# A gated convolution layer on one Trainium2 core: six tiles for the output weights, fourteen seven-product pairs, and sums made early

## The chip, the cores and the metric

The kernel runs on one core of one Trainium2 chip. The metric is the device time of one execution, in microseconds. The core has five engines that matter here: TensorE (PE) multiplies, VectorE (DVE) and ScalarE (ACT) work element by element, GpSimd (POOL) does small sums, and SyncE (SP) issues most of the transfers. A queue of an engine is worked off in the order in which it was written.

## What is computed

```python
D, E, T = 2048, 4096, 256            # model width, branch width, tokens; one sequence, one layer
h = rmsnorm(x, norm_g)
shift, scale, gate = split(silu(c) @ ada_w + ada_b, 3)
h = h * (1 + scale) + shift
b_gate, c_gate, v, g = split(h @ w_in, 4)        # w_in: D x 4E
u = causal_depthwise_conv(c_gate * v, conv_w)    # three taps
y = b_gate * u * silu(g)
out = rmsnorm(x + gate * (y @ w_out), final_g)   # w_out: E x D
```

All inputs and outputs are float32.

## The kernel before

**Products.** A float32 product is made of three matmuls in the type fp32r. Both operands are split into a high part (a cast, on ScalarE) and a low part (what the cast left out, a subtraction on VectorE), and high times high, high times low and low times high are added up. In the code a weight block `raw` gives `hi` (`split_hi`, line 380) and `lo` (`split_lo`, line 385). All weights are streamed from HBM in tiles of 128 x 2048 (1 MB). Three kinds of tile, called raw, hi and lo, exist three times each; `w_tile(kind, name)` hands them out in turn, and an engine that writes one waits until the last reader of its former contents is done. How tiles are handed out, and the order of each engine's instructions, is settled when the program is built: a list scheduler goes by the written order and by times of its own, and may put an instruction that it takes for ready ahead of an earlier one.

**Stages.** In the first 376 us the first half of the input projection runs while the adaptive norm's scale and shift are computed (matmuls `mm_s`). From 376 to 724 us the second half runs (`mm_b`): 8 groups of two channel tiles by 4 quarters (`QUARTERS`) by 2 blocks of `w_in`, 64 blocks of 48 matmuls. In its first half the gate's share of `ada_w` is streamed beside it, one `gate_piece` a block, and summed on VectorE and, over the partitions, on POOL; the bias comes into the two `gates` tiles at the stage's start, and POOL adds the sums to it. After the fourth quarter of a group `y` is ready, split into high and low part (`split_y`), as pair `ct // 2` of the 16 pairs of channel tiles.

**The output stage** multiplies `y` by `w_out` and runs from 724 us to the end. The first 1024 columns go first (`columns`, tiles `wide`), for the pairs in the given order; then the next 1024 columns (`halves`) for 12 of the pairs, while the last 8 channel tiles (`LAST`, two groups of `EP = 4`) are handled 512 columns at a time, the last 512 columns with the weights multiplied by the gate beforehand (`gated_piece`), so that their sum can go straight to the final row. A plain pair is 8 block products, two channel tiles by two token tiles by two column blocks of 512: 24 matmuls of 512 columns.

**Seven products.** For the pairs in `SEVEN` a scheme with seven block products takes the place of the eight, 21 matmuls. It needs sums of token blocks (`token_forms`, made when the pair's `y` is) and sums of weight blocks, which `seven` makes on VectorE (lines 837, 843 and 844) in a tile of kind lo. Such a pair uses two raw, two hi and two lo tiles: its own blocks 1 to 3 and the four sums. Its intermediate products pile up in the banks `p1`, `p6` and `p75`, and `gather` adds them up behind the last such pair. Before the change there are 6 such pairs in the first half (10 to 15) and 4 in the second (10 to 13). `tc.add_manual_dep` puts a pair's first sum behind the low part of the pair in front.

In the output stage the raw weights and the sums lie in the three tiles of kind lo, and the low parts in those of kind raw. The large buffer `big`, which holds the tokens until the last input product, then takes the residual `x` (`xr`), the row of final gains (`fg`) and a scratch row (`u2`); `load_ends` issues these loads behind pairs 4 to 6 of the order. At the end `residual`, `weighted` and `finish` apply gate, residual and norm and store the rows.

Of the kernel before, what the change touches and what calls it, by code (L numbers as in the profile page):

```python
# [13 lines left out]
P = 128  # L14
D = 2048
# [102 lines left out]
def short_conv_layer(ctx: ExitStack, tc: tile.TileContext, x, c, norm_g, ada_w, ada_b, w_in, conv_w, w_out, final_g, out):  # L118
# [553 lines left out]
    for j in range(2):  # L672
        nc.sync.dma_start(
            gates[j].rearrange("p a f -> p (a f)"),
            ada_b[0:1, 2 * D + j * 1024 : 2 * D + (j + 1) * 1024].partition_broadcast(P),
        )

    def gate(dc):
        return gates[dc // 2][:, dc % 2, :]

    gate_todo = [(dc, j) for dc in range(4) for j in range(0, KT, 2)]
    gacc = [None]
# [35 lines left out]
    ended_silu = [None]  # L718

    def token_forms(pair, u):  # L720

        sums = zs[0][:, 1].rearrange("p a (b f) -> p (a b) f", f=P)
        a11, a12 = u[:, 0, 0:P], u[:, 1, 0:P]
        a21, a22 = u[:, 0, P:T], u[:, 1, P:T]
        s1n, s2, s3, s4 = (sums[:, j] for j in range(4))
        nc.vector.scalar_tensor_tensor(out=s1n, in0=a21, scalar=-1.0, in1=a22, op0=ALU.mult, op1=ALU.subtract)
        nc.vector.scalar_tensor_tensor(out=s2, in0=s1n, scalar=-1.0, in1=a11, op0=ALU.mult, op1=ALU.subtract)
        nc.vector.tensor_tensor(out=s3, in0=a11, in1=a21, op=ALU.subtract)
        nc.vector.tensor_tensor(out=s4, in0=a12, in1=s2, op=ALU.subtract)
# [10 lines left out]
        nc.vector.tensor_tensor(out=lo, in0=sums, in1=hi.bitcast(F32), op=ALU.subtract)  # L740

    for ct in range(NS, NCT, 2):
        for q in QUARTERS:
            bank = psum.tile([P, CT, T], F32, tag="mm", name="mm_b")[:, 0:2]
            col = q * E + ct * P
            for kp in range(0, KT, KP):
# [6 lines left out]
                for m in range(2):  # L753
                    for i in range(KP):
                        k = kp + i
                        o = slice((i * 2 + m) * P, (i * 2 + m + 1) * P)
                        for j in range(3):
                            product(bank[:, m, :], hi[:, o], lo[:, o], k, j, k == 0 and j == 0, m == 0, k == KT - 1 and j == 2)
                gate_piece()
            z = zs[q // 2][:, q % 2]  # L760
            if q == 1:
                nc.scalar.copy(z, bank)
# [9 lines left out]
            else:  # L772
                nc.vector.tensor_tensor(out=u, in0=bank, in1=u, op=ALU.mult)
                split_y(ys[ct // 2], u)
                if ct // 2 in SEVEN:
                    token_forms(ct // 2, u)
    while gate_todo:
        gate_piece()


    W = 512
    big = hpool.tile([P, 3 * D + W], F32, tag="big", name="big")
    xr = big[:, 0 : TT * D].rearrange("p (t f) -> p t f", t=TT)
    fg = big[:, TT * D : 3 * D]
    u2 = big[:, 3 * D :]
    ends = [z.rearrange("p a b f -> p (a b f)").rearrange("p (h f) -> p h f", h=2) for z in zs]

    def load_ends(n):

        if 0 <= n < TT:  # L790
            nc.sync.dma_start(xr[:, n, :], x[n * P : (n + 1) * P, :])
        elif n == TT:
# [9 lines left out]
    def load_o(raw, e0, ne, c0, n):  # L802
        nc.sync.dma_start(
            raw.rearrange("p (k f) -> p k f", k=ne),
            w_out[0, e0 * P : (e0 + ne) * P, c0 : c0 + n].rearrange("(k p) f -> p k f", p=P),
        )

    def y_parts(ct, t):
        return [ys[ct // 2][:, ct % 2, h, t * P : (t + 1) * P] for h in range(2)]
# [6 lines left out]
    def residual(t, c0, n, src, pr):  # L816


        r = xr[:, t, c0 : c0 + n]
        g = gates[c0 // 1024].rearrange("p a f -> p (a f)")[:, c0 % 1024 : c0 % 1024 + n]  # L820
        nc.vector.tensor_tensor(out=pr, in0=src, in1=g, op=ALU.mult)
        nc.vector.tensor_tensor(out=r, in0=r, in1=pr, op=ALU.add)

    def weighted(t, c0, n, pr, at):


        r = xr[:, t, c0 : c0 + n]
# [3 lines left out]
    def seven(j, raw, bank, p1, p6, p75, opens, last):  # L831


        sums = w_tile("lo", "sums_o")
        hi, lo = hi_tile(), lo_tile("raw")
        b, s, bh, bl = (v.rearrange("p (b f) -> p b f", f=W) for v in (raw, sums, hi, lo))
        first = nc.vector.tensor_tensor(
            out=s[:, 0:2], in0=b[:, 1:3], in1=b[:, 0:1].to_broadcast([P, 2, W]), op=ALU.subtract
        )
        if last_low[0] is not None:  # L840
            tc.add_manual_dep(first.ins, last_low[0].ins.name, after, reason="the pair in front comes first")
        nc.scalar.copy(bh[:, 1:4], b[:, 1:4])
        nc.vector.tensor_tensor(out=s[:, 2], in0=b[:, 2], in1=s[:, 0], op=ALU.add)
        all_sums = nc.vector.tensor_tensor(out=s[:, 3], in0=b[:, 3], in1=s[:, 2], op=ALU.subtract)
        low = nc.vector.tensor_tensor(out=bl[:, 1:4], in0=b[:, 1:4], in1=bh[:, 1:4].bitcast(F32), op=ALU.subtract)
        tc.add_manual_dep(low.ins, all_sums.ins.name, after, reason="the sums' cast runs beside the low part")
        sh, sl = (v.rearrange("p (b f) -> p b f", f=W) for v in split(sums, SLOT, "raw"))
# [19 lines left out]
        add(ends[0][:, 0], p75[:, 1], u2)  # L867
        add(ends[1][:, 0], p75[:, 1], ends[1][:, 1])

    def columns(c0, order, sevens, bank, p1, p6, p75, whole, loads=None):  # L870
# [26 lines left out]
    def wide_bank(name):  # L897
# [2 lines left out]
    p75 = wide_bank("mm_7")  # L900
    wide = [wide_bank("mm_w") for _ in range(TT)]
    columns(
        0, (0, 1, 10, 2, 11, 3, 12, 4, 13, 5, 14, 6, 15, 7, 8, 9), SEVEN,
        lambda t, d: wide[t][:, d], *extra_banks(), p75, True, load_ends,
    )
    for t in range(TT):
        c = ends[t].rearrange("p h f -> p (h f)")
# [7 lines left out]
    def finish(t):  # L915
# [3 lines left out]
        nc.vector.reciprocal(fs, fs)  # L919
        for c0, n, vector in ((0, 512, True), (512, 512, False), (1536, 512, True), (1024, 512, False)):  # L920
            dd = slice(c0, c0 + n)
            r = xr[:, t, dd]
            if c0 == 1536:
                nc.vector.scalar_tensor_tensor(out=r, in0=po[t], scalar=fs, in1=fg[:, dd], op0=ALU.mult, op1=ALU.mult)
            elif vector:
# [2 lines left out]
                nc.scalar.activation(r, r, AF.Copy, scale=fs)  # L928
            nc.sync.dma_start(out[t * P : (t + 1) * P, dd], r)

    halves = [wide_bank("mm_o") for _ in range(2)]
    p75 = wide_bank("mm_7")
    LAST = (3, 4)
# [17 lines left out]
    def move(t):  # L951
# [5 lines left out]
        nc.vector.tensor_tensor(out=c, in0=c, in1=xr[:, t, 3 * W : 4 * W], op=ALU.add)  # L957
        nc.scalar.copy(po[t], c)

    def gated_piece(ep):  # L960
        raw = w_tile("lo", "raw_o")
        load_o(raw, ep * EP, EP, 3 * W, W)
        raw3 = raw.rearrange("p (k f) -> p k f", k=EP)
        nc.vector.tensor_tensor(out=raw3, in0=raw3, in1=gate(3).unsqueeze(1).to_broadcast([P, EP, W]), op=ALU.mult)
        return raw

    def third(t):
# [53 lines left out]
```

## Time and profile before

| | us |
|---|---|
| median of three runs | 901.92 (900.71, 901.92, 902.15) |
| span of the profiled execution, first to last instruction | 898.9 |
| its time outside the span | not listed; the span is 3.0 below the median |
| PE busy | 886.5 |
| DVE busy | 674.4 |
| ACT busy | 484.0 |
| POOL busy | 95.6 |

In the rows quoted below, PE is TensorE's matmuls, DVE is VectorE, ACT ScalarE, SPq the queue of transfers that SyncE issues; L385 is line 385 of the kernel. A row of a group gives line, engine, operation, what is written and read with its shape, how often, then the busy time in us, the mean of one in ns, and the idle time ahead of it with what ended it. A row of waits gives who waited for whom, in total, how often, and the longest. A row of the chain and of the timeline gives start and length in us; a matmul's length there contains a modelled end, so that one matmul's price is read from start to start. A row of the chain of work that ended last has how many matmuls followed each other without a gap.

### The profile page before, as it was taken

What the parts mean: (1) busy time and instruction counts of PE and PEld (TensorE: products, weight loads), DVE (VectorE), ACT (ScalarE), POOL (GpSimd) and SP (SyncE); (2) the same over time, 40 slices, a digit from 0 to 9 for tenths busy, and PEclk for the clock granted to TensorE, in tenths of its full rate; (3) what the DMA queues carried; (4) which work ended last, traced back from release to release, by engine and by line L of the source; (5) the groups of instructions that cost most, each with busy time, mean ns of one, the idle gap of its engine ahead of it and who ended that gap; (6) DMA issues with size and microseconds to landing.
All of it is one profiled execution on the core that took longest, in us unless ns stands there. A gap on an engine that the chain in (4) does not pass through costs nothing.

```text
span 898.9 us, 16428 instructions
## 1 busy us (share of the span) xinstructions
PE 886.5 (99%) x6989; PEld 849.7 (95%) x6989; DVE 674.4 (75%) x667; ACT 484.0 (54%) x430; POOL 95.6 (11%) x107
## 2 busy tenths in 40 slices
PE   7999999999999999999999999999999999999996
PEld 4999999999999999999999999999999988888885
DVE  5899988899888866755965677565555578879896
ACT  6768866665558856644433444443434445554543
POOL 0000001010000134024134103410000000000000
PEclk9999999999999999999999999999999999999998
DMA  9999999999998597687888789766666476674662
GB/s 309 369 369 368 369 336 361 347 365 367 372 318 291 167 277 231 196 266 244 278 246 242 252 273 274 233 207 204 193 188 188 141 290 224 192 276 126 202 234 94
DMA packets 160250, 235.53 MB, mean 262 GB/s; under 512 B 7028, under 2 KB 105924, under 8 KB 159792
## 3 DMA queue, kind: packets, MB, share of 16 engines
q1 hardware_dynamic: 156368, 226.52, 76.8%
q0 software_dynamic: 3680, 7.92, 3.2%
q8 instruction: 55, 0.90, 0.4%
q14 instruction: 19, 0.16, 0.0%
q10 hardware_dynamic: 128, 0.04, 0.0%
HBM read 224.49 MB, written 2.10 MB: 252 GB/s over the span
## 4 chain that ended last, share of the span: by engine, by line
PE 97%; DMA 2%; SPq 0%; ACT 0%; issue 0%; ACTq 0%; DVE 0%
PE mm_s L545 39%; PE mm_b L545 39%; PE mm_w L814 7%; PE mm_o L814 7%; PE mm L814 4%; DMA at<-in_ada_w_dram 2%; PE sum L418 0%; SPq L240 0%; PE tp_g L530 0%; PE tp_g L526 0%; ACT big L928 0%; ACTq L1017 0%; ACT fs L918 0%; ACT z L991 0%; DVE fs L919 0%
## 5 line engine op out<-in xcount | busy, mean ns | idle before, releaser
L545 PE MATMUL mm_b<-hT,hi 128*128 128x256 f32 x2048 | 348.2, 276 | 0.0
L545 PE MATMUL mm_s<-hT,hi 128*128 128x256 f32 x2048 | 335.6, 277 | 0.0
L545 PEld LDWEIGHTS mm_b<-hT,hi 128*128 128x128 f32 x2048 | 308.1, 188 | 0.0
L545 PEld LDWEIGHTS mm_s<-hT,hi 128*128 128x128 f32 x2048 | 299.0, 188 | 0.2
L545 PE MATMUL mm_b<-hT,lo 128*128 128x256 f32 x1024 | 282.6, 276 | 0.0
L545 PE MATMUL mm_s<-hT,lo 128*128 128x256 f32 x1024 | 261.3, 276 | 0.0
L385 DVE TENSOR_TENSOR lo<-raw,hi 128x2048 fp32r<-128x2048 f32 (+1 forms) x66 | 152.4, 2311 | 103.1 <-ACT hi L380 102.6
L380 ACT CAST hi<-raw 128x2048 fp32r<-128x2048 f32 (+1 forms) x66 | 123.7, 1874 | 192.7 <-PE mm_b L545 146.6
L545 PEld LDWEIGHTS mm_b<-hT,lo 128*128 128x128 f32 x1024 | 192.2, 188 | 0.0
L545 PEld LDWEIGHTS mm_s<-hT,lo 128*128 128x128 f32 x1024 | 182.4, 188 | 0.0
L385 DVE TENSOR_TENSOR lo<-raw_s,hi 128x2048 fp32r<-128x2048 f32 (+1 forms) x80 | 149.1, 1871 | 34.7 <-ACT hi L380 34.2
L380 ACT CAST hi<-raw_s 128x2048 fp32r<-128x2048 f32 (+2 forms) x81 | 124.1, 1541 | 61.7 <-PE mm_s L545 46.7
L515 DVE SCALAR_TENSOR_TENSOR gv<-at,silu_c,gv 128x512 f32<-128x512 f32 x105 | 79.0, 752 | 5.5 <-DMA at<-in_ada_w_dram 3.6
L568 ACT COPY acc<-mm_s 128x1024 f32<-128x1024 f32 x54 | 54.6, 1012 | 37.0 <-PE mm_s L545 37.0
L385 DVE TENSOR_TENSOR lo<-raw_o,hi 128x2048 fp32r<-128x2048 f32 x22 | 50.4, 2290 | 22.9 <-ACT hi L380 22.9
L380 ACT CAST hi<-raw_o 128x2048 fp32r<-128x2048 f32 x22 | 42.0, 1908 | 45.8 <-DMA raw_o<-in_sc_w_out_dram 12.3
L814 PE MATMUL mm_w<-hi,y 128*128 128x512 f32 x184 | 58.8, 389 | 0.0
L710 POOL TENSOR_TENSOR gacc<-gacc,z 128x512 f32<-128x512 f32 x28 | 45.6, 1628 | 106.8 <-DMA z<-gacc 106.8
L814 PE MATMUL mm_o<-hi,y 128*128 128x512 f32 x176 | 55.3, 389 | 0.0
L704 DVE SCALAR_TENSOR_TENSOR gacc<-at_g,silu_c,gacc 128x512 f32<-128x512 f32 x60 | 46.9, 782 | 6.0 <-DMA at_g<-in_ada_w_dram 4.8
L814 PEld LDWEIGHTS mm_w<-hi,y 128*128 128x128 f32 x184 | 34.5, 188 | 7.2
L582 ACT COPY mm_s<-acc 128x1024 f32<-128x1024 f32 x38 | 38.6, 1017 | 2.6 <-DVE acc L571 1.8
(161 smaller groups left out, 670.8 us busy)
## 6 DMA issues: line engine op xcount, KB each, us to landing
raw<-in_sc_w_in_dram SPq DMA_DIRECT2D x64, 1024.0 KB, 5.8
raw_s<-in_sc_w_in_dram SPq DMA_DIRECT2D x47, 1024.0 KB, 7.9
raw_o<-in_sc_w_out_dram SPq DMA_DIRECT2D x32, 1024.0 KB, 5.2
at<-in_ada_w_dram SPq DMA_DIRECT2D x126, 256.0 KB, 7.8
raw_s<-in_sc_w_in_dram SPq DMA_DIRECT2D x33, 512.0 KB, 7.3
at_g<-in_ada_w_dram SPq DMA_DIRECT2D x32, 512.0 KB, 8.0
x<-in_x_dram SPq DMA_DIRECT2D x4, 512.0 KB, 6.2
big<-in_x_dram SPq DMA_DIRECT2D x2, 1024.0 KB, 8.2
```

The source lines that it names most:

```text
L380: nc.scalar.copy(hi[:, :n], raw[:, :n])
L385: last_low[0] = nc.vector.tensor_tensor(out=lo[:, :n], in0=raw[:, :n], in1=hi[:, :n].bitcast(F32), op=ALU.subtract)
L515: nc.vector.scalar_tensor_tensor(out=gv, in0=at4[:, i], scalar=c_k, in1=gv, op0=ALU.mult, op1=ALU.add)
L545: mm = last_mm[0] = nc.tensor.matmul(dst, w, h[k], start=begins and left, stop=ends, skip_group_check=True)
L568: nc.scalar.copy(acc[ch, q], bank)
L582: nc.scalar.copy(bank, acc[ch, q])
L704: nc.vector.scalar_tensor_tensor(out=ga, in0=at3[:, i, :], scalar=s, in1=ga, op0=ALU.mult, op1=ALU.add)
L710: nc.gpsimd.tensor_tensor(out=ga, in0=ga, in1=turned, op=ALU.add)
L814: nc.tensor.matmul(dst, y[a], b, start=opens and i == 0, stop=ends and i == 2, skip_group_check=True)
```

## The change

- `SEVEN` becomes 8 to 15 in the first half, and `SEVEN_2`, 10 to 15, holds in the second: 14 seven-product pairs for 10. The orders of the pairs change. The token forms of pairs 8 and 9 lie in the two gate tiles.
- For that the gate leaves these tiles: it is kept as a row in HBM (`gate_row`), POOL's last sum of each quarter is added to it by an accumulating transfer, and `load_gate` fetches it in two halves, at the 11th and 14th pair (counted from 0) of the first half.
- In the first 1024 columns raw weights and sums go round six tiles (`wide_ring`): the three of kind lo, and three more in `big`, up to the 13th pair. From then `x` (first 1024 columns) and `fg` are loaded there. In the second half there are four (`next_ring`), the fourth in `big`, until twelve were handed out; then the second half of `x` is loaded there, at the 8th pair.
- `early_weights`, called behind each of the 64 blocks of the second input stage, makes the weight sums of pairs 10 to 15 for the second half (blocks 35, 39, ... 55) and the two gated pieces (blocks 59 and 62, the gate's last quarter being fetched at 58): load, VectorE, and a store to HBM on ACT's queue one block later. In the output stage they are loaded, with blocks 1 to 3 of the raw weights; the sums and the multiplication by the gate go out of that stage.
- `LAST` is (2, 3) and no longer (3, 4).

```diff
-    gates = [slot([P, 2, 512], f"gate{j}") for j in range(2)]
+    gate_slots = [slot([P, 2, 4, P], f"gate{j}", F32R) for j in range(2)]
...
+    gate_row = dram.tile([1, D], F32, tag="gate_row", name="gate_row")
+    nc.gpsimd.dma_start(gate_row, ada_b[0:1, 2 * D : 3 * D])
...
+    def load_gate(j):
+        c0 = j * 1024
+        nc.sync.dma_start(gate_columns(c0, 1024), gate_row[0:1, c0 : c0 + 1024].partition_broadcast(P))
...
-            nc.gpsimd.tensor_tensor(out=gate(dc), in0=ga, in1=gate(dc), op=ALU.add)
+            nc.gpsimd.dma_start(gate_row[0:1, dc * 512 : (dc + 1) * 512], ga[0:1], accum_op=ALU.add)
...
-    SEVEN = range(10, 16)
+    SEVEN = range(8, 16)
+    SEVEN_2 = range(10, 16)
...
-        if pair < 14:
+        if pair < 10:
+            form = gate_slots[pair - 8]
+            hi, lo = form[:, 0], form[:, 1]
+        elif pair < 14:
...
+    LAST = (2, 3)
+    EARLY = {35 + 4 * i: j for i, j in enumerate(SEVEN_2)}
+    EARLY.update({58: "gate", 59: ("gated", LAST[0]), 62: ("gated", LAST[1])})
+    def sums_of(b, s):
+        yield nc.vector.tensor_tensor(
+            out=s[:, 0:2], in0=b[:, 1:3], in1=b[:, 0:1].to_broadcast([P, 2, W]), op=ALU.subtract
+        )
+        yield nc.vector.tensor_tensor(out=s[:, 2], in0=b[:, 2], in1=s[:, 0], op=ALU.add)
+        yield nc.vector.tensor_tensor(out=s[:, 3], in0=b[:, 3], in1=s[:, 2], op=ALU.subtract)
+    def early_weights():
+        while to_store:
+            unit, sums = to_store.pop()
+            made[unit] = dram.tile([P, SLOT], F32, tag=f"made{len(made)}", name="made")
+            nc.scalar.dma_start(made[unit], sums)
+        unit = EARLY.get(passed[0])
+        passed[0] += 1
+        if unit is None:
+            return
+        if unit == "gate":
+            nc.sync.dma_start(turned, gate_row[0:1, 3 * W : 4 * W].partition_broadcast(P))
+            return
+        raw, sums = raw_tile("raw_u"), w_tile("lo", "sums_u")
+        blocks, out = (v.rearrange("p (b f) -> p b f", f=W) for v in (raw, sums))
+        if not isinstance(unit, int):
+            load_o(raw, unit[1] * EP, EP, 3 * W, W)
+            nc.vector.tensor_tensor(out=out, in0=blocks, in1=turned.unsqueeze(1).to_broadcast([P, EP, W]), op=ALU.mult)
+        else:
+            load_o(raw, 2 * unit, 2, 2 * W, 2 * W)
+            list(sums_of(blocks, out))
+        to_store.append((unit, sums))
...
                 gate_piece()
+                early_weights()
...
+    places6 = [None] * 3 + [big[:, i * SLOT : (i + 1) * SLOT] for i in range(3)]
+    taken, ending = [0], [False]
+    def wide_ring(name):
+        i = taken[0] % 6 if not ending[0] else 0
+        taken[0] += 1
+        return w_tile("lo", name) if places6[i] is None else places6[i]
     def load_ends(n):
+        ending[0] = n >= AT_END
+        if n == AT_END - 2:
+            load_gate(0)
+        elif n == AT_END:
+            load_x(0)
+        elif n == AT_END + 1:
             nc.sync.dma_start(fg, final_g.rearrange("(o d) -> o d", o=1).partition_broadcast(P))
+            load_gate(1)
...
+    AT_END = 13
...
-            raw = w_tile("raw" if n == 0 and c0 == 0 else "lo", "raw_o")
-            load_o(raw, 2 * j, 2, c0, 2 * W)
+            raw = w_tile("raw", "raw_o") if n == 0 and c0 == 0 else ring("raw_o")
+            ready = c0 > 0 and j in made
+            if ready:
+                blocks = raw.rearrange("p (b f) -> p b f", f=W)
+                e = 2 * j * P
+                nc.sync.dma_start(blocks[:, 1], w_out[0, e : e + P, c0 + W : c0 + 2 * W])
+                nc.sync.dma_start(blocks[:, 2:4].rearrange("p b f -> p (b f)"), w_out[0, e + P : e + 2 * P, c0 : c0 + 2 * W])
+            else:
+                load_o(raw, 2 * j, 2, c0, 2 * W)
             if loads:
-                loads(n - 4)
+                loads(n)
             if j in sevens:
-                seven(j, raw, bank, p1, p6, p75, j == sevens[0], j == sevens[-1])
+                sums = ring("sums_o")
+                if ready:
+                    nc.sync.dma_start(sums, made[j])
+                seven(j, raw, sums, ready, bank, p1, p6, p75, j == sevens[0], j == sevens[-1])
...
-        0, (0, 1, 10, 2, 11, 3, 12, 4, 13, 5, 14, 6, 15, 7, 8, 9), SEVEN,
+        0, (0, 1, 8, 2, 9, 3, 10, 4, 11, 5, 12, 13, 6, 14, 15, 7), SEVEN,
...
+    AT_X = 8
+    def next_ring(name):
+        i = taken[0] % 4
+        taken[0] += 1
+        return big[:, SLOT : 2 * SLOT] if i == 3 and taken[0] <= 12 else w_tile("lo", name)
...
-        2 * W, (0, 1, 2, 10, 3, 11, 4, 12, 5, 13, 14, 15), SEVEN[0:4],
-        lambda t, d: halves[d][:, t], *po, p75, False,
+        2 * W, (0, 1, 10, 2, 11, 3, 12, 13, 8, 14, 15, 9), SEVEN_2,
+        lambda t, d: halves[d][:, t], *po, p75, False, lambda n: load_x(1) if n == AT_X else None, next_ring,
...
     def gated_piece(ep):
         raw = w_tile("lo", "raw_o")
-        load_o(raw, ep * EP, EP, 3 * W, W)
-        raw3 = raw.rearrange("p (k f) -> p k f", k=EP)
-        nc.vector.tensor_tensor(out=raw3, in0=raw3, in1=gate(3).unsqueeze(1).to_broadcast([P, EP, W]), op=ALU.mult)
+        nc.sync.dma_start(raw, made["gated", ep])
         return raw
```

More of the change, by code (lines that the diff above doesn't have):

```diff
@@ L776, in short_conv_layer, with xr, load_x @@
                     token_forms(ct // 2, u)
+    early_weights()
     while gate_todo:
         gate_piece()
-    W = 512
     big = hpool.tile([P, 3 * D + W], F32, tag="big", name="big")
-    xr = big[:, 0 : TT * D].rearrange("p (t f) -> p t f", t=TT)
+    xh = big[:, 0 : TT * D].rearrange("p (h t f) -> p h t f", h=2, t=TT)
+    HD = D // 2
+    def xr(t, c0, n):
+        return xh[:, c0 // HD, t, c0 % HD : c0 % HD + n]
+    def load_x(h):
+        for t in range(TT):
+            nc.sync.dma_start(xh[:, h, t], x[t * P : (t + 1) * P, h * HD : (h + 1) * HD])
     fg = big[:, TT * D : 3 * D]
@@ L816, in residual, with seven @@
     def residual(t, c0, n, src, pr):
-        r = xr[:, t, c0 : c0 + n]
-        g = gates[c0 // 1024].rearrange("p a f -> p (a f)")[:, c0 % 1024 : c0 % 1024 + n]
-        nc.vector.tensor_tensor(out=pr, in0=src, in1=g, op=ALU.mult)
+        r = xr(t, c0, n)
+        nc.vector.tensor_tensor(out=pr, in0=src, in1=gate_columns(c0, n), op=ALU.mult)
         nc.vector.tensor_tensor(out=r, in0=r, in1=pr, op=ALU.add)
     def weighted(t, c0, n, pr, at):
-        r = xr[:, t, c0 : c0 + n]
+        r = xr(t, c0, n)
         nc.scalar.activation(pr, r, AF.Square, scale=D**-0.5, accum_out=fsq[:, t, at : at + 1])
         nc.vector.tensor_tensor(out=r, in0=r, in1=fg[:, c0 : c0 + n], op=ALU.mult)
-    def seven(j, raw, bank, p1, p6, p75, opens, last):
-        sums = w_tile("lo", "sums_o")
+    def seven(j, raw, sums, ready, bank, p1, p6, p75, opens, last):
         hi, lo = hi_tile(), lo_tile("raw")
         b, s, bh, bl = (v.rearrange("p (b f) -> p b f", f=W) for v in (raw, sums, hi, lo))
[L837 to L844, printed above, removed]
+        steps = [] if ready else sums_of(b, s)
+        all_sums = last_low[0]
+        for i, step in enumerate(steps):
+            if i == 0:
+                tc.add_manual_dep(step.ins, last_low[0].ins.name, after, reason="the pair in front comes first")
+                nc.scalar.copy(bh[:, 1:4], b[:, 1:4])
+            all_sums = step
+        if ready:
+            nc.scalar.copy(bh[:, 1:4], b[:, 1:4])
         low = nc.vector.tensor_tensor(out=bl[:, 1:4], in0=b[:, 1:4], in1=bh[:, 1:4].bitcast(F32), op=ALU.subtract)
@@ L902, in short_conv_layer @@
     columns(
-        0, (0, 1, 10, 2, 11, 3, 12, 4, 13, 5, 14, 6, 15, 7, 8, 9), SEVEN,
-        lambda t, d: wide[t][:, d], *extra_banks(), p75, True, load_ends,
+        0, (0, 1, 8, 2, 9, 3, 10, 4, 11, 5, 12, 13, 6, 14, 15, 7), SEVEN,
+        lambda t, d: wide[t][:, d], *extra_banks(), p75, True, load_ends, wide_ring,
     )
@@ L921, in finish @@
             dd = slice(c0, c0 + n)
-            r = xr[:, t, dd]
+            r = xr(t, c0, n)
             if c0 == 1536:
@@ L956, in move @@
         nc.vector.tensor_tensor(out=c, in0=c, in1=gate(3), op=ALU.mult)
-        nc.vector.tensor_tensor(out=c, in0=c, in1=xr[:, t, 3 * W : 4 * W], op=ALU.add)
+        nc.vector.tensor_tensor(out=c, in0=c, in1=xr(t, 3 * W, W), op=ALU.add)
         nc.scalar.copy(po[t], c)
```

33 lines of the change are left out of this document (17 added, 16 removed).

## The prediction

> **What bounds the kernel now.** I read the page first, then what TensorE waited for, then the chain that ended last.
>
> ```profile
> span 898.9 us, 16428 instructions
> PE 886.5 (99%) x6989; PEld 849.7 (95%) x6989; DVE 674.4 (75%) x667; ACT 484.0 (54%) x430; POOL 95.6 (11%) x107
> PE   7999999999999999999999999999999999999996
> DVE  5899988899888866755965677565555578879896
> raw_o<-in_sc_w_out_dram SPq DMA_DIRECT2D x32, 1024.0 KB, 5.2
> ```
>
> ```profile
> PE tp_v L274 <- DMA rows<-in_c_dram: 4.2, 1, 4.2
> PE sum L418 <- DMA at<-in_ada_w_dram: 0.4, 1, 0.4
> PE tp_x L335 <- ACT xs L341: 0.3, 1, 0.3
> PE sum L418 <- DVE mod L448: 0.3, 1, 0.3
> ```
>
> TensorE is busy for 886.5 of 898.9 us, and its waits (the second fence is all of them) are 5.2 us in total, all of the start-up. From the first product to the last nothing keeps it waiting, so only fewer matmuls, or a new stall, can move the time. VectorE is the next engine: the fifth row of the page shows it at 8 to 9 tenths in the last eight slices, which are the output stage that the change rewrites.
>
> ```profile
> 375.88 348.16 PE mm_b L545 x3072
> 724.04 10.89 PE mm_w L814 x48
> 790.27 16.79 PE mm_w L814 x74
> 807.07 16.32 PE mm_o L814 x72
> 880.81 10.89 PE mm L814 x48
> ```
>
> The output stage runs from 724.04 to 880.81 + 10.89 = 891.70 us. One matmul of 512 columns costs 10.89 / 48 = 0.2269 us from start to start. In the first 1024 columns the kernel issues 10 plain pairs of 24 matmuls and 6 seven-product pairs of 21, 366 in all: 366 x 0.2269 = 83.04 us, and the chain has 807.07 - 724.04 = 83.03. In the second half 8 x 24 + 4 x 21 + 48 + 48 = 372 give 84.4 against 84.6. So the matmul count alone gives the length, without a gap. A pair costs 5.44 us plain and 4.76 us with seven products.
>
> **The gain.** Seven-product pairs go from 6 to 8 in the first half and from 4 to 6 in the second: 360 + 366 matmuls instead of 366 + 372. Twelve fewer are 12 x 0.2269 = 2.72 us, or 0.30%. Nothing else lies on the path, since the tail behind the last matmul is not edited. The rest of the working asks what of the 2.72 us is given back.
>
> **VectorE in the first half.** The rows are mean durations in the output stage.
>
> ```profile
> L385 DVE TENSOR_TENSOR lo<-raw_o,hi 128x2048 fp32r<-128x2048 f32 x17 | 38.9, 2289 | 12.8 <-ACT hi L380 12.8
> L385 DVE TENSOR_TENSOR lo<-sums_o,hi 128x2048 fp32r<-128x2048 f32 x7 | 16.0, 2291 | 2.3 <-ACT hi L380 2.3
> L380 ACT CAST hi<-sums_o 128x2048 fp32r<-128x2048 f32 x6 | 11.5, 1911 | 12.8 <-DVE sums_o L844 12.8
> L845 DVE TENSOR_TENSOR lo<-raw_o,hi 128x1536 fp32r<-128x1536 f32 x6 | 10.5, 1750 | 0.0
> L837 DVE TENSOR_TENSOR sums_o<-raw_o 128x1024 f32<-128x1024 f32 x6 | 7.3, 1219 | 0.0
> L964 DVE TENSOR_TENSOR raw_o<-raw_o,gate 128x2048 f32<-128x2048 f32 x2 | 4.6, 2284 | 0.0
> L844 DVE TENSOR_TENSOR sums_o<-raw_o,sums_o 128x512 f32<-128x512 f32 x6 | 4.1, 691 | 0.2
> L843 DVE TENSOR_TENSOR sums_o<-raw_o,sums_o 128x512 f32<-128x512 f32 x6 | 4.1, 691 | 0.2
> ```
>
> A seven-product pair costs VectorE 1.22 + 0.69 + 0.69 + 1.75 + 2.29 = 6.64 us against 4.76 us of TensorE; a plain pair 2.29 against 5.44. Alternated, 8.93 stands against 10.20, and the kernel before runs so without a gap. The new order has pairs 12, 13 and 14, 15 back to back: 12, 13, 6, 14, 15 are 4 x 6.64 + 2.29 = 28.9 us of VectorE. These are the rows around pair 15 of today:
>
> ```profile
> 775.57 0.39 PE L814 MATMUL mm<-hi,y 128*128 128x512 f32 x1
> 776.24 1.91 ACT L380 CAST hi<-raw_o 128x2048 fp32r<-128x2048 f32 x1 [1.78 <-DMA raw_o<-in_sc_w_out_dram]
> 778.18 2.29 DVE L385 TENSOR_TENSOR lo<-raw_o,hi 128x2048 fp32r<-128x2048 f32 x1 [1.39 <-ACT hi L380]
> 779.34 1.48 ACT L842 CAST hi<-raw_o 128x1536 fp32r<-128x1536 f32 x1 [1.20 <-DMA raw_o<-in_sc_w_out_dram]
> 780.39 1.22 DVE L837 TENSOR_TENSOR sums_o<-raw_o 128x1024 f32<-128x1024 f32 x1
> 785.11 2.29 DVE L385 TENSOR_TENSOR lo<-sums_o,hi 128x2048 fp32r<-128x2048 f32 x1 [0.38 <-ACT hi L380]
> 785.77 0.39 PE L814 MATMUL mm<-hi,y 128*128 128x512 f32 x1
> 786.22 0.39 PE L814 MATMUL mm<-lo,y 128*128 128x512 f32 x1
> 787.83 0.58 ACT L864 COPY z<-mm 128x512 f32<-128x512 f32 x1
> 794.51 0.68 DVE L863 TENSOR_TENSOR z<-mm,z 128x512 f32<-128x512 f32 x1
> ```
>
> The sums start at 780.39, 5.38 us ahead of the pair's first matmul (785.77), and with its wait the pair takes VectorE 785.11 + 2.29 - 780.39 = 7.01 us. From such a start, the last low part of 12, 13, 6, 14, 15 is ready 28.9 - 5.4 = 23.5 us (6.64 a pair) to 4 x 7.01 + 2.29 - 5.38 = 24.9 us (7.01 a pair) behind pair 12's first matmul. TensorE wants it after 4.76 + 4.76 + 5.44 + 4.76 + 2.04 (nine matmuls of pair 15) = 21.8 us: it is 1.7 to 3.1 us late. Two things shrink that. The cast at 776.24 waited for its load, though the last matmul on its tile had ended when pair 14 began (775.57 + 0.39 = 775.96): 0.3 us, which six tiles give back. And TensorE's queue has matmuls of high parts in front: pair 15 begins at 785.77 and its first low one comes at 786.22, two later. The second tile of a pair has eight of them, 1.8 us, of which two are 0.45. So the stall lies between 0 (1.7 less 0.3 and 1.8) and 2.8 us (3.1 less 0.3), and with today's two in front between 0.95 and 2.35. I take 0.5, nearer the low end, because the trace shows this remedy at work: pair 6 begins at 785.77 - 24 x 0.2269 = 780.32, its low part is ready at 778.18 + 2.29 = 780.47, and TensorE has no gap.
>
> **The gather.** Its copy and four adds empty the bank that the second half opens with. Today they lie between 787.83 and 795.19, 7.4 us, with two low parts in between, and three plain pairs cover them. In the new order only pair 7 does, 5.44 us. Bare, the work is 0.58 + 4 x 0.69 = 3.3 us. So 0 to 1.9 us; I take 0.1, nearer the bare work, since gather stands ahead of the low parts in the program.
>
> **The work made early.** Six sets of sums (2.60 us), two gated pieces (2.28) and two sets of forms go to VectorE under the mm_b products. The first row of the second fence is that stage from the time when the gate pieces are nearly done (busy TensorE, weight loads, VectorE, ACT, POOL; clock, DMA share, GB/s).
>
> ```profile
> 593.52 0.69 DVE L773 TENSOR_TENSOR z<-mm_b,z 128x512 f32<-128x512 f32 x1 [0.32 <-PE mm_b L545]
> 598.16 0.68 DVE L740 TENSOR_TENSOR form<-z,form 128x512 fp32r<-128x512 f32 x1
> ```
>
> ```profile
> 550.00:724.00 174.00, 174.00 (x1537) 174.00 (x1536) 97.59 (x84) 73.95 (x58) 16.02 (x17) 1.00 0.65 201
> 728.00:732.00 4.00, 4.00 (x19) 3.34 (x18) 2.67 (x4) 2.42 (x2) 0.00 (x0) 1.00 1.02 432
> 800.00:804.00 4.00, 4.00 (x20) 3.30 (x19) 0.86 (x2) 1.91 (x1) 0.00 (x0) 1.00 1.01 344
> ```
>
> There VectorE has 76 us free of 174, and 6 x 2.60 + 2 x 2.28 = 20 us come in. Eight loads and eight stores of 1.05 MB add 16.8 MB, 97 GB/s on 201, against 344 to 432 when the DMA engines are full. The extra unit takes one of three lo tiles, so for two blocks of 348.16 / 64 = 5.44 us the low part has one block to be made instead of two. The heaviest such block, the end of a quarter with forms, is 593.52 to 598.84, a low part included: 5.3 us. It fits by 0.1, and the high parts' matmuls run ahead; behind it would wait the next block's products. I take 0.1 for all eight units, with 0 and 8 x 0.3 as ends. The stores sit on ACT's queue behind sums that are a block old. At the stage's end, pair 1's load has to wait for the last block but one, 724.04 - 5.44 = 718.6; + 5.2 to land + 1.91 + 2.29 = 728.0, wanted at 724.04 + 5.44 = 729.5: no cost. POOL loses an add per gate quarter and gets a small DMA; the gate is only wanted 130 us later.
>
> **The second half.** With sums ready a pair costs VectorE 1.75 + 2.29 = 4.04 us, under TensorE's 4.76 even back to back, and the two gated multiplications leave. No cost. What is late next is the loads: a ready pair brings 0.75 + 1 tiles, 1.84 MB. From pair 12 to pair 15 (12, 13, 8, 14, 15) and 9 with the second half of x, 4 x 1.84 + 3 x 1.05 = 10.5 MB in 4 x 4.76 + 2 x 5.44 = 29.9 us: 351 GB/s. Loads of w_out alone ran at 344 (800 to 804); x and the row of gains, whose rows are longer, at 432 (728 to 732). The sums are stored in long rows as well, so I mix: 4 x (0.79 / 344 + 1.05 / 432) + 2 x 1.05 / 344 + 1.05 / 432 = 27.4 us, 2.5 us to spare. I take 0, and the rival below for the other end. The Trainium skill, "DMA: Bandwidth & Descriptors", section Specifications, puts a core's share of HBM at about 358 GB/s; by that the stretch would be 98% full, and the time nearer the second rival's 903.4. The 432 GB/s of this trace goes against the rule.
>
> **Sum.** -2.72 + 0.5 + 0.1 + 0.1 = -2.0 us. The profiled execution has only its span, 898.9, which lies 3.0 us under the median of 901.92; I take the difference over to the median: **899.9 us**. A measurement here tells about 0.2% (1.8 us) from no change, so the forecast is only just faster.
>
> **Rivals.**
> 1. VectorE gives the gain back. The scheduler, which fixes the order of TensorE's queue beforehand, puts only the two high matmuls of today in front, so that the back-to-back pairs cost 1.8 us (in the upper half of 0.95 to 2.35), 1.3 more than I took, and the low parts go in among the gather's adds as today: 0.4 us more. 899.9 + 1.7 = 901.6, no change. For it: today's gather. Against: the deeper ring.
> 2. Slower: the load of x. It overwrites the tile that pair 13's sums leave, 6.6 us behind pair 12's first matmul (its high tile is free after nine matmuls, 2.04, and 0.4; + 1.91 + 2.29), and it is issued on SP in the middle of the fullest stretch. If it goes in written order, behind pair 8's load, the loads of pair 14 stand behind it: 6.6 + 2.1 latency (5.2 less 1.05 MB at 344) + 2.4 (x) + 2.3 + 2.4 = 15.8, + 1.91 + 2.29 = 20.0 for sums wanted at 4.76 + 4.76 + 5.44 + 2.04 = 17.0. That is 3.0 us, and for pairs 15 and 9 behind it, three tiles deep, I add 0.5: 3.5 us. 899.9 + 3.5 = 903.4. It decides when the slack of 2.5 us in this stretch is used up.
>
> ```profile
> 722.78 0.37 SPq L803 DMA_DIRECT2D raw_o<-in_sc_w_out_dram  x1
> 723.39 0.82 SPq L791 DMA_DIRECT2D big<-in_x_dram  x2
> 730.04 13.85 SPq L803 DMA_DIRECT2D raw_o<-in_sc_w_out_dram  x3
> ```
>
> Against it: SP's order today isn't the written one. The loads of x stand behind the fifth and sixth pair's load in the program, and they went out at 723.39, ahead of both (730.04); so a load that is ready can pass one that waits.
>
> **How the numbers follow.** Forecast 0.60 (899.2 to 900.8; below 900.1 in 0.50 of it), rival 1 0.25, rival 2 0.15. Faster 0.50, same 0.10 + 0.25 = 0.35, slower 0.15. The range starts at 901.9 - 2.7 less 0.4 for the spread of the runs, 898.8, and reaches past rival 1 to 902.6; beyond it lies most of rival 2.
>
> **What would show it.** Right: TensorE with 726 matmuls in the output stage, 164.7 us and a gap of about half a microsecond at pair 15; no wait of TensorE under mm_b; the casts of the first half no longer waiting for raw_o. Wrong: waits of TensorE for sums' low parts of over 2 us in the first half (rival 1), or ACT casts waiting for sums_o or raw_o loads at pairs 14 and 15 of the second (rival 2), or gaps under mm_b.

## The result and the profile after

The changed kernel takes 916.39 us (915.4 to 917.38) against 901.7 us before: 1.0163 times as long, 95% interval 1.0152 to 1.0175. The forecast was 899.9, with a range to 902.6. The page of the changed kernel:

```profile
span 915.2 us, 16520 instructions
PE 888.6 (97%) x6977; PEld 849.9 (93%) x6977; DVE 695.4 (76%) x693; ACT 490.5 (54%) x436; POOL 88.0 (10%) x108
PE   7999999999999999999999999949999999999996
```

Its span is 915.2 - 898.9 = 16.3 us longer. TensorE does its twelve matmuls less (6977 against 6989), and yet one slice of the 40, the 27th (595 to 618 us), is at 4 tenths, where the row of before has 9s. That is under the second input stage, not in the output stage. TensorE's waits name it:

```profile
PE mm_b L545 <- ACT hi L380: 11.4, 1, 11.4
PE mm_b L545 <- DVE lo L385: 1.5, 1, 1.5
PE mm L888 <- DVE lo L918: 1.0, 2, 0.6
```

The three stages of the changed kernel, from first matmul to first matmul (length, then busy time of PE, PEld, DVE, ACT and POOL, the granted clock, the share of the DMA engines and GB/s):

```profile
376.90:740.20 363.30, 350.34 (x3074) 349.85 (x3073) 238.59 (x221) 145.69 (x114) 48.93 (x55) 0.98 0.82 259
740.20:824.70 84.50, 83.16 (x362) 67.16 (x361) 75.42 (x60) 45.16 (x28) 0.00 (x0) 1.00 0.72 247
824.70:907.90 83.20, 83.20 (x367) 68.36 (x365) 66.22 (x54) 43.02 (x36) 0.00 (x0) 1.00 0.68 237
```

Before, measured the same way on the timeline (375.72, 723.88, 806.90, end 891.69), these stages took 348.2, 83.0 and 84.8 us. The last figure of each kernel holds some 0.2 us of the last matmul's modelled end. So the second input stage lost 15.1 us, the first half of the output stage lost 1.5 although it has six matmuls less, and the second half won 1.6. Another 1.2 us lie ahead of 376.9; runs below, with the same code up to there, start that stage anywhere from 375.8 to 377.1, so it is scatter.

What stands behind the 11.4 us, read backwards. ScalarE's cast of a block, and the first matmul that needs it, with the idle time in front:

```profile
604.15 1.90 ACT L380 CAST hi<-raw 128x2048 fp32r<-128x2048 f32 x1 [19.73 <-DMA raw<-in_sc_w_in_dram]
606.10 0.80 PE L545 MATMUL mm_b<-hT,hi 128*128 128x256 f32 x2 [11.43 <-ACT hi L380]
```

The cast waited for its weights. SP's queue issues them; this is its timeline, and what it waited for ahead of the load at L786, which fetches the gate's last quarter for the gated pieces:

```profile
575.93 0.37 SPq L755 DMA_DIRECT2D raw_u<-in_sc_w_out_dram  x1
596.25 0.34 SPq L786 DMA_DIRECT2D z<-gate_row  x1
596.70 12.07 SPq L804 DMA_DIRECT2D raw<-in_sc_w_in_dram  x4
```

```profile
SPq L786 <- DMA z<-gacc: 15.9, 1, 15.9
SPq L786 <- DMA gate_row<-gacc: 3.8, 1, 3.8
```

From 576.3 to 596.25 SP issued nothing. It stood at the gate's load, which waited 19.7 us for POOL's fold of that quarter over the partitions and its addition to the row in HBM:

```profile
542.97 0.56 POOL L715 DMA_DIRECT2D z<-gacc  x1 [48.24 <-DVE gacc L711]
593.92 0.82 POOL L719 DMA_DIRECT2D gate_row<-gacc  x1 [0.30 <-POOL gacc L717]
```

The program asks for this load at block 58. A queue is worked off in the order that the list scheduler gave it, not in the order of the program text, and in SP's order the load stands ahead of the weights of block 40. Nothing else would have held these back for long: with the load on another queue they went out at 577.05 (first run below). Here they were issued at 596.70, cast at 604.15, and their first matmuls came at 606.10 and 608.42 in place of 594.5. Behind the gap the granted clock is low as well:

```profile
606.00:611.40 5.40, 3.77 (x16) 3.48 (x17) 5.22 (x4) 1.94 (x2) 0.00 (x0) 0.51 1.04 374
```

It is at 0.51 from 606.0 to 611.4. So the 15.1 us are 11.4 + 1.5 of waits and about 2 of slow clock (busy PE is 350.3 us in this stage against 348.2). The Trainium skill, "TensorE: Matmul & The Clock Gate", Part 1, says that an idle window of about 3.4 us takes the clock to half and that as long a busy one gives it back; this gap of 11.4 us, with 0.51 behind it, fits the first. Shorter waits had half the clock behind them too (last section).

### The profile page after: what moved, and what is told of

It is laid out like the page before. It is cut to its first block, busy times and chain, and to the rows that moved or that the text cites. A ratio compares the mean times of both kernels' runs of the same rounds, so it can differ in the third digit from the quotient of the medians.

```text
span 915.2 us, 16520 instructions
## 1 busy us (share of the span) xinstructions
PE 888.6 (97%) x6977; PEld 849.9 (93%) x6977; DVE 695.4 (76%) x693; ACT 490.5 (54%) x436; POOL 88.0 (10%) x108
## 4 chain that ended last, share of the span: by engine, by line
PE 79%; DMA 11%; DVE 4%; ACT 2%; POOL 2%; issue 1%; SPq 0%; ACTq 0%; POOLq 0%; DVEq 0%
PE mm_s L545 38%; PE mm_b L545 27%; PE mm_o L888 6%; PE mm L888 4%; DMA z<-gacc 3%; PE mm_w L888 3%; DMA at_g<-in_ada_w_dram 3%; DVE lo L385 2%; DMA at<-in_ada_w_dram 2%; ACT hi L380 2%; POOL gacc L717 1%; DMA raw_o<-in_sc_w_out_dram 1%; DMA raw<-in_sc_w_in_dram 1%; POOL z L715 0%; DVE gacc L711 0%
## 5 line engine op out<-in xcount | busy, mean ns | idle before, releaser
L545 PE MATMUL mm_b<-hT,hi 128*128 128x256 f32 x2048 | 349.9, 277 | 11.4 <-ACT hi L380 11.4
L888 PE MATMUL mm_w<-hi,y 128*128 128x512 f32 x160 | 51.4, 390 | 0.3 <-ACT hi L380 0.3
L711 DVE SCALAR_TENSOR_TENSOR gacc<-at_g,silu_c,gacc 128x512 f32<-128x512 f32 x60 | 45.0, 749 | 7.4 <-DMA at_g<-in_ada_w_dram 6.3
L888 PE MATMUL mm_o<-hi,y 128*128 128x512 f32 x152 | 48.3, 389 | 0.0
L380 ACT CAST hi<-raw_o 128x2048 fp32r<-128x2048 f32 x14 | 26.7, 1909 | 22.1 <-DMA raw_o<-in_sc_w_out_dram 16.8
L385 DVE TENSOR_TENSOR lo<-raw_o,hi 128x2048 fp32r<-128x2048 f32 x14 | 32.1, 2289 | 6.8 <-ACT hi L380 6.7
L888 PEld LDWEIGHTS mm_w<-hi,y 128*128 128x128 f32 x160 | 30.0, 188 | 6.9 <-ACT hi L380 0.7
```

The source lines that it names most:

```text
L380: nc.scalar.copy(hi[:, :n], raw[:, :n])
L385: last_low[0] = nc.vector.tensor_tensor(out=lo[:, :n], in0=raw[:, :n], in1=hi[:, :n].bitcast(F32), op=ALU.subtract)
L545: mm = last_mm[0] = nc.tensor.matmul(dst, w, h[k], start=begins and left, stop=ends, skip_group_check=True)
L888: nc.tensor.matmul(dst, y[a], b, start=opens and i == 0, stop=ends and i == 2, skip_group_check=True)
```

## The experiments

**What makes the gap under mm_b.** Theory 1 is the reading above: one load that waits stops SP's queue. Theory 2 is that the eight early units take tiles and DMA time, so that blocks come late anyway.

The load on another queue, POOL's, which is idle there:

```diff
-            nc.sync.dma_start(turned, gate_row[0:1, 3 * W : 4 * W].partition_broadcast(P))
+            nc.gpsimd.dma_start(turned, gate_row[0:1, 3 * W : 4 * W].partition_broadcast(P))
```

> The changed kernel with one word different: the load of the gate's last quarter for the two gated pieces is issued on POOL's queue and not on SP's. Theory 1 (SP's queue stands still): that load waits for POOL's fold of the last gate quarter (to 594.7 us), was put ahead of block 40's weights, and holds them back. Then mm_b goes back from 363.3 to about 348.2 us, no wait of TensorE under it, time 916.4 - 15 = 901.4 (900.4 to 902.4). Theory 2 (tiles): the eight early units take raw and lo tiles and DMA time, and the blocks come late for that. Then the gap under mm_b stays, at 912 or more.

Measured: 901.48 us, 1.0003 of the kernel before (0.9994 to 1.0012). SP's order is the same but for this one load. Block 40's weights, the first of four here, and then the three stages:

```profile
577.05 13.91 SPq L804 DMA_DIRECT2D raw<-in_sc_w_in_dram  x4
```

```profile
375.80:723.90 348.10, 348.10 (x3074) 348.10 (x3073) 238.81 (x221) 146.13 (x114) 53.38 (x56) 1.00 0.85 271
723.90:808.10 84.20, 82.78 (x362) 67.22 (x361) 75.54 (x60) 45.16 (x28) 0.00 (x0) 1.00 0.73 247
808.10:891.80 83.70, 83.70 (x367) 68.37 (x366) 66.19 (x54) 43.04 (x36) 0.00 (x0) 1.00 0.67 235
```

PE is busy for all of the 348.10 us, with all eight early units beside it. Theory 1 told the time to 0.1 us; Theory 2 is out as the cause.

The early sums taken away, the load left on SP:

```diff
-    EARLY = {35 + 4 * i: j for i, j in enumerate(SEVEN_2)}
+    EARLY = {}
```

> The changed kernel without the six early weight sums (they are made in the output stage); the gate's load and the two gated pieces stay early. Theory 1: SP still waits for the fold, now ahead of block 41, which TensorE wants 5.4 us later: a gap of 6 to 8 us and slow clock behind it, the output stage 0 to 3 us longer for the sums; 909 to 913. Theory 2: most of the tiles' load is gone, the gap under mm_b with it; 900 to 904.

Measured: 910.13 us, 1.0101 (1.0079 to 1.0122). SP's wait, and then the second input stage and the second half of the output stage:

```profile
SPq L786 <- DMA z<-gacc: 14.8, 1, 14.8
```

```profile
375.80:728.50 352.70, 350.36 (x3074) 349.96 (x3073) 225.82 (x205) 145.42 (x114) 53.30 (x55) 1.00 0.74 232
813.80:902.20 88.40, 85.48 (x367) 68.03 (x366) 81.00 (x72) 42.46 (x36) 0.00 (x0) 1.00 0.52 178
```

The wait is there without a single early sum. It costs 4.6 us here (2.3 of listed waits of TensorE, the rest slow clock behind them) and not the 6 to 8 I expected, one block later and with the fold a little sooner. The second half of the output stage shows what the early sums are worth in this order of the pairs: 88.4 us with the sums made in the stage, 83.7 with them made early.

The wait alone, put into the kernel before. A 2 KB store of the finished gate quarter stands ahead of block 40's weights; it moves nothing that anyone needs:

```diff
+        wait[0] = nc.sync.dma_start(scrap, gate(3)[0:1, :]) if passed[0] == 40 else None
...
+                if wait[0] is not None:
+                    tc.add_manual_dep(load.ins, wait[0].ins.name, after, reason="behind the wait")
```

> The kernel before with one thing added: a store of 2 KB of the finished gate's last quarter to HBM, on SP's queue ahead of block 40's weights; no early units. Theory 1: SP waits for POOL's last add (591.1 us), block 40's weights land at about 597 and its first matmul comes at 599 to 601 in place of 593.5; 901.7 + 6 to 10 = 908 to 912. Theory 2: no early unit, so no gap; 901.7 within 1 us.

Measured: 910.8 us, 1.0105 (1.0091 to 1.0119). The store in SP's timeline, what it waited for, and TensorE's longest wait under `mm_b`:

```profile
588.64 0.31 SPq L750 DMA_DIRECT2D scrap<-gate  x1
```

```profile
SPq L750 <- POOL gate L712: 23.2, 1, 23.2
```

```profile
PE mm_b L545 <- ACT hi L380: 4.1, 1, 4.1
```

One idle 2 KB transfer, 9.5 us (910.8 against the 901.32 of the kernel before, measured beside it). With that the cause is shown from both sides: take the wait away and the loss goes, add it alone and most of it comes. It is less than 15.1, and SP stood still until 588.64 here, not until 596.25.

The load on SP again, but held behind the weights of block 58, the place that the program names:

```diff
+            tc.add_manual_dep(g.ins, block_load[0].ins.name, after, reason="not ahead of its block")
```

> The changed kernel with the gate's load still on SP's queue, but held behind the weights of block 58, where the program asks for it. If the place in the queue is the cause, the fold is over by then (611 us in the run with POOL's queue) and nothing waits: 901.5 (900.5 to 902.5), no gap under mm_b. If a load on SP that follows POOL's transfers costs by itself, a gap of some us comes at block 59 to 61 and the time is over 904.

Measured: 901.59 us, 1.0004 (0.9996 to 1.0013). It went out at 673.60, behind block 58's weights and with nothing to wait for, and the second input stage is without a gap:

```profile
673.60 0.34 SPq L787 DMA_DIRECT2D z<-gate_row  x1
```

```profile
376.20:724.40 348.20, 348.20 (x3075) 348.20 (x3074) 238.53 (x221) 145.72 (x114) 50.91 (x55) 1.00 0.85 271
```

So it isn't the queue or the kind of load that costs, only its place. The changed kernel without its accident is as fast as the kernel before, which leaves the second question.

**Where the 2.72 us of fewer matmuls went.** In the run with the load on POOL the first half takes 84.2 us where 360 matmuls need 81.7, the second 83.7 (0.2 of it the modelled end) where 366 need 83.0. Theory A: VectorE falls behind where two seven-product pairs follow each other. Theory B: the loads of gate, x and gains near the end of the first half come between. VectorE and TensorE there, pairs 12 to 15:

```profile
770.12 1.22 DVE L769 TENSOR_TENSOR sums_o<-raw_o 128x1024 f32<-128x1024 f32 x1
777.06 1.22 DVE L769 TENSOR_TENSOR big<-big 128x1024 f32<-128x1024 f32 x1
779.65 1.75 DVE L918 TENSOR_TENSOR lo<-big,hi 128x1536 fp32r<-128x1536 f32 x1
780.70 0.39 PE L888 MATMUL mm_w<-hi,y 128*128 128x512 f32 x1
781.45 0.50 PE L888 MATMUL mm<-lo,y 128*128 128x512 f32 x1 [0.37 <-DVE lo L918]
797.52 0.50 PE L888 MATMUL mm<-lo,y 128*128 128x512 f32 x1 [0.65 <-DVE lo L918]
800.49 0.51 PE L888 MATMUL mm_w<-hi,y 128*128 128x512 f32 x1 [0.40 <-ACT hi L380]
798.54 1.91 ACT L380 CAST hi<-raw_o 128x2048 fp32r<-128x2048 f32 x1 [0.73 <-DMA raw_o<-in_sc_w_out_dram]
```

Pair 12 takes VectorE from 770.12 to 777.06, 6.94 us, and pair 13's low part is ready at 781.40, when TensorE has been waiting since its matmul of 780.70. From start to start these three places lose 0.53, 0.82 and 0.56 us. The first two wait for VectorE. The third is of another kind: TensorE waits for pair 7's cast, which had itself waited 0.73 us for its load. That load went out at 793.23, just as a low part of VectorE ended (790.91 + 2.29 = 793.20), so VectorE most likely stands behind it as well, by the tile that it freed.

The old six pairs in the first half, alternating, all else as with the load on POOL (`SEVEN = range(10, 16)`, the old order):

> The changed kernel with the gate's load on POOL, and in the first 1024 columns the old six seven-product pairs in the old order (alternating); six tiles, early units and second half as changed. Theory A (VectorE falls behind where two seven-product pairs follow each other): 366 matmuls without a gap, 83.0 us for the first half against 84.2 with eight; 901.5 - 1.2 = 900.3. Theory B (the new loads of gate, x and gains between pairs 11 and 14 make the tiles late): gaps stay near the end of the first half, 901.5 or more.

Measured: 900.72 us, 0.9995 (0.9986 to 1.0004); the first half takes 83.7 us. Seven pairs, each behind a plain one:

```diff
-    SEVEN = range(8, 16)
+    SEVEN = range(9, 16)
-        0, (0, 1, 8, 2, 9, 3, 10, 4, 11, 5, 12, 13, 6, 14, 15, 7), SEVEN,
+        0, (0, 1, 9, 2, 10, 3, 11, 4, 12, 5, 13, 6, 14, 7, 15, 8), SEVEN,
```

> The changed kernel with the gate's load on POOL, and in the first 1024 columns seven seven-product pairs (9 to 15), each behind a plain one. Theory A: 363 matmuls x 0.2269 = 82.4 us, no gap at pairs 13 and 15; 901.5 - 1.8 = 899.7. The gather has one pair of cover, as in the changed kernel, at most 0.5 us. Theory B: gaps at the pairs 13 to 15 stay, 901 or more.

Measured: 900.23 us, 0.9989 (0.9980 to 0.9998), the first version whose interval lies below 1, by little. First half, and all that TensorE waits for in the output stage:

```profile
725.20:808.30 83.10, 83.04 (x365) 68.04 (x365) 71.39 (x56) 43.68 (x27) 0.00 (x0) 1.00 0.74 254
```

```profile
PE mm_o L888 <- DVE lo L385: 0.4, 1, 0.4
```

The gaps at pairs 13 and 15 are gone, and x, gains and gate are still loaded there; that is for A. It does not part the order from the count, since this run has one seven-product pair less and no doublet; eight pairs in strict alternation were not run. Both runs came in some 0.5 us above A's forecast: 83.7 us for 366 matmuls and 83.1 for 363 are 0.7 over the bare matmuls. In each, 0.6 of that lies at two places at the half's start (731 and 739), where a low part from VectorE comes 0.2 us late, too little to be listed as a wait.

The other way to relieve VectorE, eight pairs but the sums of 13 and 15 premade for the first half too:

```diff
+    EARLY.update({37: (13, 0), 41: (15, 0)})
```

> The changed kernel with the gate's load on POOL, and the first half's sums of pairs 13 and 15 made early too (blocks 37 and 41, ten early units), order and eight pairs as changed. Theory A: VectorE has 2.6 us less at each of the two places; the gaps of 0.5 at pair 13 and 1.4 at pair 15 go, first half 81.7 to 82.0, time 901.5 - 2.3 = 899.2 if the two more units cost nothing under mm_b. Theory B: the gaps stay or grow, as 0.8 MB more is loaded for each; 901.5 or more.

Measured: 915.41 us, 1.0168 (1.0143 to 1.0194): a clear miss of Theory A's number. Its first two stages and TensorE's waits in them, and one of ScalarE's casts ahead of the longest:

```profile
376.20:732.50 356.30, 352.08 (x3074) 351.29 (x3073) 243.53 (x227) 146.13 (x114) 50.12 (x53) 0.99 0.85 275
732.50:818.60 86.10, 82.62 (x363) 67.50 (x362) 72.67 (x55) 46.75 (x29) 0.00 (x0) 1.00 0.80 274
```

```profile
PE mm_b L545 <- DVE lo L385: 2.5, 3, 1.8
PE mm L889 <- ACT hi L918: 2.1, 1, 2.1
PE mm_b L545 <- ACT hi L380: 1.7, 1, 1.7
PE mm L889 <- DVE lo L385: 1.4, 1, 1.4
```

```profile
816.77 1.47 ACT L918 CAST hi<-raw_o 128x1536 fp32r<-128x1536 f32 x1 [1.31 <-DMA raw_o<-in_sc_w_out_dram]
```

Two units more, at every second block instead of every fourth, cost 8 us under mm_b: what Theory 2 said is true at that density, and not at the change's. Whether tiles or DMA time are short there was not taken apart. And in the first half the gaps are not gone but moved and grown, one now at a cast that waits for its load. So relief of VectorE by more loads does not help there; B holds for this version.

Three tiles and not six in the first half, on top of the seven pairs:

```diff
-        return w_tile("lo", name) if places6[i] is None else places6[i]
+        return w_tile("lo", name)
```

> The run with seven pairs in the first half, with three tiles and not six for its raw weights and sums; x and the gains then load at the start of the half, as in the kernel before. If the loads set the pace of the first half, casts wait for raw_o and gaps of over 1 us come: 901.2 or more. If VectorE alone does, which the kernel before speaks for (three tiles, pairs alternating, no gap), it stays at 900.2 within 0.6.

Measured: 904.65 us, 1.0042 (1.0030 to 1.0053). The longest waits of the casts in the first half are for loads, 15.1 us where the run with six tiles had 8.2, and TensorE waits there (its longest below, 3.4 us in all):

```profile
ACT hi L380 <- DMA raw_o<-in_sc_w_out_dram: 15.1, 5, 7.6
```

```profile
PE mm_w L888 <- DVE lo L385: 1.8, 2, 1.6
```

The ring is worth 4.4 us here (904.65 less 900.23). I had expected none, from the kernel before, which needs only three; but here SP waits 9.0 us at the stage's start for the store of an early unit's sums, and x, gains and a gate half are loaded at 723.5 to 725.2, ahead of the next weights (730.4); so three don't do. Which of the two weighs more was not tested.

The second half in another order (0, 10, 1, 11, 2, 12, 3, 13, 8, 14, 15, 9):

> The run with seven pairs in the first half, and in the second half the order 0, 10, 1, 11, 2, 12, 3, 13, 8, 14, 15, 9, with one place where two seven-product pairs meet, not two. If the small gaps of the second half (84.0 us for 366 matmuls, 83.0 without a gap) come from 12, 13 and 14, 15, about half goes: 900.2 - 0.5 = 899.7. If the start of the half is what is tight (bank p75 and pair 10's loads straight behind pair 0), a new gap of 0.5 to 2 us comes at pair 10: 900.7 to 902.

Measured: 901.98 us, 1.0007 (0.9998 to 1.0015), with a new wait of the size that the second guess gave, but not at pair 10. It comes at the first low matmul of pair 1, the plain pair behind it, and what VectorE does up to that low part (which starts at 817.89) is the first half's sum with the residual (L894, L895):

```profile
815.62 2.35 DVE L895 TENSOR_TENSOR big<-big,z 128x1024 f32<-128x1024 f32 x2
820.22 0.50 PE L888 MATMUL mm_o<-lo,y 128*128 128x512 f32 x1 [1.29 <-DVE lo L385]
```

Around this wait the clock stays up: PE is busy for 5.71 of the 7.00 us from 815 to 822, at a granted clock of 1.00. The start of the half is what is tight, on VectorE; of the two orders the change's is the better one.

The version that the runs point to has the seven alternating pairs and the load held behind block 58:

> The version the runs point to: seven pairs in the first half, alternating, the gate's load held on SP behind block 58's weights, the rest as changed. First half 83.1 us as in the run with seven pairs, second 83.1 as in the run with the load held: 899.5 (899.0 to 900.5), 0.1 to 0.2% under the kernel before. If the second half's gap of 0.5 us of the run with seven pairs belongs to the seven pairs, 900.2.

Measured: 900.15 us, 0.9983 (0.9974 to 0.9992). It is 1.1 us under the kernel before in the medians (901.25, measured beside it) and 16 us under the changed one. That is inside the forecast's range, but at its second figure, 900.2. From the second input stage on no wait of TensorE is listed; the two halves of the output stage:

```profile
725.10:808.00 82.90, 82.86 (x365) 68.03 (x365) 71.39 (x56) 43.70 (x27) 0.00 (x0) 1.00 0.75 253
808.00:891.50 83.50, 83.50 (x367) 68.44 (x365) 66.00 (x54) 43.03 (x36) 0.00 (x0) 1.00 0.67 235
```

## Why the prediction was wrong

- **The gain.** Right as a count: 6989 - 6977 = 12 matmuls.
- **The work made early** is the step that failed. Of the gate it said "POOL loses an add per gate quarter and gets a small DMA; the gate is only wanted 130 us later", and put 0.1 us on all eight units, with 2.4 us as the far end. It priced POOL's side and left out the transfer that the change adds on SP, `turned` from `gate_row`, what that waits for, and what is queued behind it. It took the written place, block 58, for the place in the queue. It is 18 blocks earlier, where the fold (51.8 us from 542.97 to 594.7, seven rounds of two transfers and an add) had 20 us to go. Cost: 15.1 us. The units themselves cost nothing (348.10 busy of 348.10 with the load on POOL). Gaps under mm_b stood among the signs of being wrong, but only tiles and VectorE's time had been weighed as their reason.
- The clue was in the prediction: SP's order "isn't the written one", shown by x passing two loads that waited. I used it only against rival 2. What lets a ready load go ahead also lets one go ahead that is thought to be ready; what the scheduler took for ready here is not in any trace.
- **VectorE in the first half.** I took 0.5 us from a range of 0 to 2.8; 1.9 us in three gaps and 0.6 in short pauses were measured with the load on POOL. The row ahead of it was right (a pair takes VectorE 6.94 us), the choice was wrong: I counted on more high matmuls in front. At pair 13 two ran ahead, at 778.20 to 778.65 among pair 12's, and none was left between pair 12's last (780.70) and the first low one (781.45). This is the first half of rival 1 in mechanism and size (1.8); its 0.4 us for the gather did not come.
- **The gather**, 0.1 us: right, no wait at the change of halves with the load on POOL, nor in the changed kernel.
- **The second half**, 0 us: right. 83.2 us in the changed kernel, modelled end included, for 83.0 of matmuls. Rival 2, the load of x, did not come about. The DMA engines moved 326 GB/s from 856 to 886 us, where the prediction had reckoned with 351, and TensorE was busy throughout; so the limit that it quoted was not put to the test.
- **Sum.** Without the accident the net of the rest is 0.0 (1.0003), where I said -2.0; the first half has 1.9 us of the difference. So without the accident the change would have come out where rival 1 put it (901.6), not where the forecast did.
- **A reading.** VectorE stands at 6 to 9 tenths in the last eight slices of the page before, not at 8 to 9; no term hangs on it.

## What to carry to other kernels

A new transfer has three prices: its bytes, what it waits for, and what stands behind it in its issuing queue while it waits. Look up its place in the final order of the queue, not in the program, and compare it with the time at which its data is really there; a load of 256 KB that was far from urgent cost 15 us by standing 18 blocks too early. If it depends on a slow chain on another engine, issue it from that engine's queue, or pin it behind a load that comes late enough; each of the two took the loss away here.

When two engines are near balance, look at the order of the work and not only at its sum. In the first half VectorE had 8 x 6.64 + 8 x 2.29 = 71.4 us of work beside 81.7 of matmuls, and the two doublets still cost 1.4 us in waits for it. Seven seven-product pairs in alternation were faster than eight with two doublets.

## What was not expected of the hardware

A wait that ends on POOL's fold has no fixed length. In the changed kernel the last quarter took 51.8 us, from 542.97 to 594.7. With the load on POOL, the same early units and an SP that did not stand still, it began at 541.98 and ended here:

```profile
606.63 0.82 POOL L719 DMA_DIRECT2D gate_row<-gacc  x1 [0.30 <-POOL gacc L717]
```

That is 65.5 us for the same seven rounds; it was 64.2 with the load held, 68.3 with two more early units, and 49.5 in the kernel before. Most of it is waits for the folding transfers, and these go with what else the DMA engines carry. From 577 to 596 us, first in the changed kernel, where SP stood still, then with the load on POOL:

```profile
577.00:596.00 19.00, 17.66 (x156) 17.46 (x155) 9.29 (x10) 2.92 (x3) 7.98 (x11) 1.00 0.32 96
577.00:596.00 19.00, 19.00 (x170) 19.00 (x170) 12.78 (x13) 6.35 (x4) 4.85 (x6) 1.00 0.99 317
```

At a DMA share of 0.32 the last three rounds waited 4.4, 2.0 and 2.2 us for their transfers, with the load on POOL 6.8, 6.7 and 5.6. So the queue that stood still shortened the wait that it stood for.

A gap of the matrix unit can cost more than itself. Behind the one of 11.4 us the clock was 0.51, and behind that of 4.1 us, in the kernel before with the wait added, it was 0.50 for 4 us; behind the one of 1.3 us it stayed at 1.00. A shorter wait than 4.1 can do it: in the run with two more early units one of 2.1 us ended at 818.3, and this came behind it (the first row is that of the 4.1 us):

```profile
600.00:604.00 4.00, 4.00 (x19) 4.00 (x20) 3.87 (x6) 2.94 (x3) 0.00 (x0) 0.50 0.71 222
819.00:822.00 3.00, 3.00 (x9) 2.33 (x8) 3.00 (x3) 0.00 (x0) 0.00 (x0) 0.50 0.78 245
```

Waits of 0.5 and 1.8 us close together, in the run without early sums, had it as well (0.50 from 603.3 to 606.7); those of 0.7 and 1.6 us between 740 and 744, in the run with three tiles, had not. By the traces' records of the clock the slow stretches lasted 13.65 us in the changed kernel, 10.24 in the kernel before with the wait added, 3.41 without early sums, and 6.83 (under mm_b) and 3.41 with two more early units: whole multiples of the same 3.41.
